# A list-scheduled two-layer trunk: new matmul durations and new priorities for the planner of the second layer's mixer

## The chip, the cores and the metric

The kernel runs on one core of a Trainium2 chip. The core has five engines that work side by side, each through its own queue in order: TensorE (PE in the profile; its weight loads are PEld), VectorE (DVE), ScalarE (ACT), GpSimd (POOL), and SyncE (SP), which here only issues DMAs. They meet through semaphores. The metric is the device time of one launch in microseconds (us).

## The reference

The reference is a trunk of two residual layers over 1024 tokens of width 1024, in float32. Cut to what matters here:

```python
# layer 0
x = x + short_conv_pool_mixer(rms_norm(x), ...)
x = x + swiglu(rms_norm(x), ...)                 # 1024 -> 2816 -> 1024
# layer 1
u = rms_norm(x) @ w_in_odd      # q, three k/v pairs (compressed, selected, window), gates, conformer a/b
o = g0*attn_compressed + g1*attn_selected + g2*attn_window   # 8 heads, 2 kv groups, 8 query blocks of 128
z = a * sigmoid(b)
z = causal_dwconv(z, 31 taps) + bias
z = silu(layer_norm(z))
x = x + concat(o, z) @ w_out_odd
x = x + swiglu(rms_norm(x), ...)
```

The first statement group of layer 1, up to the product with `w_out_odd`, is what this text calls the mixer. Its compressed branch also picks, for each query block, the key blocks that the selected branch may see.

## The kernel before, in words

The program does not issue its instructions as it goes. Every call on `nc.tensor`, `nc.vector` and so on is recorded by the class `Order` as an operation with a number (`seq`, in the order of the listing), the operations it depends on and the tiles that it touches. At the end `Order.order` plays the whole list through once, engine by engine, with a duration for every operation (`_cost`) and a latency for every hand-over (`LAT`), and `issue` writes the instructions in the order found. Among the operations of an engine that are ready in this play, the one with the lowest `grp` goes first. An engine is never left idle in the play when one of its operations is ready. On the chip each engine then follows its list strictly, whatever the real times are.

Counted in the order of the listing there are 14,699 operations: 0 to 5,825 are the first layer and the norm ahead of the second, 5,826 to 10,218 the mixer, 10,219 to 14,698 the output projection, the second FFN and the store. In the mixer `nc.at(name)` gives each part a phase name:

- `cf0` to `cf3`: conformer input of 128 of the 512 channels each, two products per half (`pcb`, `pca`), result `z31[i]`
- `pa`, `pb`, `pq`: the projections to keys and values (PSUM tiles `pa`, `pbk`) and to queries (`pcq`), and what follows them on DVE, ACT and POOL (tiles `ta`, `tb`, `tq`, `stq`)
- `cmp`: the compression of keys and values
- `conv00` to `conv32`: the depthwise convolution on DVE, one instruction of 128x1024 for each tap (here called a tap; in the trace `y<-z,dwv,y`), `conv<i><third>` for channel block i
- `prep<qb>`: for query block qb the transposed queries `QQ`, the compressed branch (`sc`, `pvc`) and the selection
- `smax<qb><g>`: scores `s` of one kv group, their row maxima on DVE (`mx`), then two small POOL operations that make `nmx`, a transpose on PE (`pm`) and four ACT copies into `QQ`
- `att<qb><g>`: transposed scores `sT`, the exponential on ACT (`pT`), and the product with the values (`pv`)
- `fin<qb>`: the block's result, transposed and split into `mB`
- `cn0` to `cn6`: layer norm and swish of the convolution. `cn0` starts with a sum over all four channel blocks (`sm`) and a product with ones (`mp`), so it needs every tap; `cn6` splits the result into `mB`
- `out`: everything after.

Two things bind the order besides the data. First, tiles of one tag share a few buffers, and the play hands these out in the order of recording, not of priority: the PSUM tag `ps` (tiles `pa`, `pbk`, `pcq`, `s`, `mp`, `vps`, `rb`, `po`) has two banks, `pa` (`sT`, `pcb`) and `pb` (`pv`, `pca`) two each, and the SBUF tag `whl` (split weights and `pT`) five. Recorded behind each other are `smax41`, `mp` of `cn0`, `smax50`, `vps` of `cn1`, `smax51`: while taps are left, `mp` holds one of the two `ps` banks, and when `smax50` has given up its last bank `vps` holds the other. Second, an engine's list is strict, so an operation that waits holds up all behind it.

The lines that the change touches:

```python
op.pe = passes, hold, free(st) / 1.2
t = passes * max(hold + 2.5, free(st) / 1.2)
...
op.grp = op.seq + self.shift.get(op.phase, 0)
...
op.occ = op.dur = passes * max(hold + 2.5, load)
```

Here `hold` is the number of columns that stream through, divided by 2.4 (doubled where the play believes the clock to be at half), and `load` the number of weight columns divided by 1.2.

Of the kernel before, what the change touches and what calls it, by code (L numbers as in the profile page):

```python
# [43 lines left out]
CONV_LAST = 3  # L44
START, START_V, START_C = 2, 2, 4

SHIFT = {'cf1': 672, 'pq': 801, 'cf0': -43, 'smax30': -3276, 'conv20': 3889, 'conv21': 2209, 'cf2': 214, 'smax10': -712, 'prep0': 671, 'out': 5314, 'att10': 125, 'conv30': 1208, 'att60': 401, 'pa': -123, 'att41': 2144, 'cn3': 559, 'prep3': 81, 'att00': 758, 'att20': 74, 'att50': 15, 'smax61': -584, 'cn6': -122, 'smax70': -1663, 'smax71': -431, 'prep4': -1373, 'prep5': -230, 'cf3': 62, 'smax41': -43, 'smax40': -415, 'pb': -643, 'att61': -370, 'conv31': 760, 'att40': -99, 'att11': -239, 'conv00': 672, 'smax60': -547, 'conv22': -411, 'prep7': -479, 'cn4': -662, 'conv11': -853, 'att31': 12, 'fin4': 99, 'cmp': -34, 'fin2': -837, 'att21': 14, 'conv32': -38, 'conv01': 474, 'prep1': -211, 'conv02': -231, 'prep6': -616, 'cn1': -173, 'smax11': -290, 'fin0': 159, 'smax31': 0, 'smax01': 291, 'smax00': 366, 'conv10': -65, 'smax21': -23, 'att30': -6, 'fin7': -512, 'cn2': -18, 'fin1': -250, 'fin5': -5, 'smax20': -14, 'att71': -10, 'smax50': 563, 'cn0': -98, 'smax51': -19, 'prep2': -65, 'cn5': 10, 'att01': -8, 'fin6': 65, 'att51': -116}


C_ID, C_A, C_B, C_COS, C_SIN, C_RATIO, C_M01, C_DEL, C_END = 0, 128, 192, 256, 512, 1024, 1088, 1152, 1156  # L50
# [61 lines left out]
class Order:  # L112
# [11 lines left out]
    SPAN = 4096 / 1.2  # L124
    PHASE = 0.0
    IDLE = 0.36

    def __init__(self, tc):
        self.tc = tc
        self.ops, self.bufs, self.tags, self.boxes = [], {}, {}, {}  # L130
        for e in ("tensor", "vector", "scalar", "gpsimd", "sync"):
            setattr(self, e, _Engine(self, e))
        self.shift = SHIFT
        self.phase = None
# [86 lines left out]
    def _cost(self, op, outs, ins):  # L221
        def free(ap):
            n = 1
            for st, k in list(ap.ap)[1:]:
                n *= k
            return n

        o, n = outs[0], free(outs[0])
        in_psum = any(str(a.space).endswith("PSUM") for a in ins + outs)
        ptr = sum(1 for a in ins if free(a) == 1 and n > 1)  # L230
        if op.eng == "sync":
            size = 1
            for st, k in list(o.ap):
                size *= k
            return 60.0, size * 4 / 280.0
        if op.eng == "tensor":
            st, mv = ins[0], ins[1]
            passes, hold = 1, free(mv) / 2.4
            if st.dtype == F32:
                hold *= 2  # L240
                passes = 2 if op.name == "matmul" else 1
            op.pe = passes, hold, free(st) / 1.2
            t = passes * max(hold + 2.5, free(st) / 1.2)
            return t, t
        if op.eng == "scalar":
            t = 0.833 * n + (51 if str(ins[0].space).endswith("PSUM") else 94) + 93 * ptr + (93 if op.kw.get("accum_out") is not None else 0)
            return t, t
        if op.eng == "vector":
            big = max([n] + [free(a) for a in ins])
            if op.name == "reciprocal":  # L250
                t = 6.0 * n + 69
            elif op.name in ("tensor_scalar", "tensor_copy", "memset") and not in_psum:
                t = 0.52 * big + 69 + 60 * ptr
            else:
                t = 1.042 * big + 69 + 60 * ptr
            return t, t
        if op.kw.get("op") == ALU.pow:
            t = 300 + 165.0 * n
        elif op.name == "tensor_tensor":
            t = 147 + 2.25 * n  # L260
        elif op.name == "memset":
            t = 38 + 0.83 * n
        else:
            t = (80 if n > 256 else 150) + 3.4 * n
        return t, t


    def order(self):
        import heapq

        engines = ("tensor", "vector", "scalar", "gpsimd", "sync")
        free = {e: 0.0 for e in engines}
        fut = {e: [] for e in engines}
        av = {e: [] for e in engines}
        dma = 0.0
        act_set = [None]
        slow, span_no, active = True, 0, 0.0
        sets = {AF.Exp: "e", AF.Tanh: "e", AF.Silu: "s", AF.Gelu_apprx_tanh: "g"}

        def push(op):  # L280
            est = 0.0
            for d in op.deps:
                est = max(est, d.end + self.LAT.get((d.eng, op.eng), self.WAIT))
            for b in op.tiles:
                est = max(est, b.avail)
            op.est = est
            heapq.heappush(fut[op.eng], (est, op.grp, op.seq, op))

        def ready(op):
            op.wait -= 1  # L290
            if op.wait == 0:
                push(op)

        def alloc(q):
            while q["next"] < len(q["queue"]) and q["free"]:
                b = q["queue"][q["next"]]
                q["next"] += 1
                b.avail = heapq.heappop(q["free"])
                for op in b.waiting:
                    ready(op)  # L300

        for q in self.tags.values():
            q["free"], q["next"] = [0.0] * q["n"], 0
        for b in self.bufs.values():
            b.avail, b.left, b.end, b.waiting = None if b.tag else 0.0, 0, 0.0, []
        for op in self.ops:
            op.users = []
            op.grp = op.seq + self.shift.get(op.phase, 0)
            for b in op.tiles:
                b.left += 1  # L310
        for op in self.ops:
            op.wait = 1 + len(op.deps)
            for d in op.deps:
                d.users.append(op)
            for b in op.tiles:
                if b.avail is None:
                    op.wait += 1
                    b.waiting.append(op)
        for q in self.tags.values():
            alloc(q)  # L320
        for op in self.ops:
            ready(op)
        out = []
        while len(out) < len(self.ops):
            best = None
            for e in engines:
                if av[e]:
                    t = free[e]
                elif fut[e]:
                    t = max(free[e], fut[e][0][0])  # L330
                else:
                    continue
                if best is None or t < best[0]:
                    best = (t, e)
            t, e = best
            while fut[e] and fut[e][0][0] <= t:
                x = heapq.heappop(fut[e])
                heapq.heappush(av[e], x[1:])
            op = heapq.heappop(av[e])[-1]
            if e == "scalar":  # L340
                g = sets.get(op.args[2] if len(op.args) > 2 else None)
                if g is not None and g != act_set[0]:
                    act_set[0] = g
                    t += 1283
            if e == "tensor":

                n = int((t + self.PHASE) / self.SPAN)
                while span_no < n:
                    slow = active < 0.765 * self.SPAN if slow else active < self.IDLE * self.SPAN
                    span_no, active = span_no + 1, 0.0  # L350
                passes, hold, load = op.pe
                if slow:
                    hold *= 2
                active += passes * hold
                op.occ = op.dur = passes * max(hold + 2.5, load)
            free[e] = t + op.occ
            if e == "sync":
                dma = max(dma, t + 1300) + op.dur
                op.end = dma + 500
            else:  # L360
                op.end = t + op.dur
            out.append((t, op))
            for b in op.tiles:
                b.end = max(b.end, op.end + (self.WAIT if b.tag else 0))
                b.left -= 1
                if b.left == 0 and b.tag is not None:
                    q = self.tags[b.tag]
                    heapq.heappush(q["free"], b.end)
                    alloc(q)
            for u in op.users:  # L370
                ready(u)
        self.span = max(op.end for op in self.ops)
        return [op for t, op in out]
# [19 lines left out]
def trunk(ctx, tc, x, norm_mix, norm_ffn, ffn_gate, ffn_up, ffn_down, w_in_even, conv_a, pool_w,  # L393
# [221 lines left out]
    def sums_a(r, name, U):  # L615
# [29 lines left out]
        yield  # L645

    def seven(U, B, name, order, out, small=False):


# [946 lines left out]
```

## Time and profile before

| | |
|---|---|
| median of 3 runs | 2278.22 us (2277.93 to 2279.83) |
| the profiled execution | 2277.39 us, of which 2275.6 us are the span from first to last instruction |
| PE, DVE, ACT busy in the span | 98%, 71%, 35% |
| mixer in the trace | about 990 to 1527 us |

Each row below comes from that one profiled execution. PE busy means that a matmul is in flight, so only the rest of a window is idle time of PE. PEclk is the granted share of TensorE's clock in the window: 1.00 is 2.4 GHz throughout, 0.50 would be 1.2 GHz throughout. A wait in square brackets is idle time of the engine just before that instruction, with what ended it.

### The profile page before, as it was taken

The numbers are of one execution on the slowest core, as the hardware profiler recorded it, in microseconds if no ns is written. First come the engines' busy times: TensorE is split into PE (matmuls) and PEld (weight loads), VectorE is DVE, ScalarE is ACT, GpSimd is POOL, SyncE is SP. The second block draws the span as 40 slices with busy tenths as digits, with TensorE's granted clock in tenths as the row PEclk, the third lists the DMA queues.
The fourth block names the chain that finished last, engine by engine and source line by source line (L and its number), as shares of the span: only waits on it lengthen the run. The fifth ranks groups of instructions, "written<-read, shape, count | busy, mean of one in ns | idle before, by whom it ended". The sixth has DMA issues, their size and how long they took to land.

```text
span 2275.6 us, 27709 instructions
## 1 busy us (share of the span) xinstructions
PE 2232.2 (98%) x10831; PEld 1844.6 (81%) x10831; DVE 1611.2 (71%) x2618; ACT 798.6 (35%) x1449; POOL 79.6 (3%) x116
## 2 busy tenths in 40 slices
PE   7999999999999999999999999999999999999999
PEld 6888878888888888878887887988788888888887
DVE  6444387777777467769999998833877777774674
ACT  4222263333333212324334434641633333332220
POOL 0000000000000000101121000000000000000000
PEclk9999999999999999999999998999999999999999
DMA  5113123444437864313200000031223535368652
GB/s 173 55 56 139 65 75 109 144 154 138 167 123 278 328 236 163 126 55 92 75 19 1 1 1 1 29 121 56 84 102 122 184 120 178 128 240 325 238 195 93
DMA packets 171403, 283.93 MB, mean 125 GB/s; under 512 B 7120, under 2 KB 127880, under 8 KB 157448
## 3 DMA queue, kind: packets, MB, share of 16 engines
q1 hardware_dynamic: 171272, 282.16, 35.0%
q8 instruction: 85, 1.39, 0.3%
q14 instruction: 46, 0.38, 0.1%
HBM read 195.10 MB, written 87.03 MB: 124 GB/s over the span
## 4 chain that ended last, share of the span: by engine, by line
PE 91%; DVE 5%; ACT 1%; issue 1%; POOL 0%; DMA 0%; SPq 0%; POOLq 0%; ACTq 0%; DVEq 0%
PE pd L379 19%; PE pg L379 18%; PE pu L379 18%; PE po L379 8%; PE pv L379 4%; PE s L379 3%; PE sT L379 3%; PE pvv L379 2%; PE pp L379 2%; PE pb L379 2%; PE pcc L379 2%; PE pcq L379 2%; PE pca L379 2%; PE pcb L379 1%; PE pn L379 1%; PE pbk L379 1%
## 5 line engine op out<-in xcount | busy, mean ns | idle before, releaser
L379 PE MATMUL pd<-tw,sl 128*128 128x512 f32 x1512 | 349.7, 393 | 0.0
L379 PEld LDWEIGHTS pd<-tw,sl 128*128 128x128 f32 x1512 | 284.2, 188 | 65.2
L379 DVE SCALAR_TENSOR_TENSOR y<-z,dwv,y 128x1024 f32<-128x1024 f32 x120 | 154.1, 1284 | 0.8
L379 PEld LDWEIGHTS pv<-V,pT 128*128 128x128 f32 x1056 | 142.8, 193 | 6.6 <-ACT pT L379 0.6
L379 DVE TENSOR_TENSOR xf<-pd,xf 128x512 f32<-128x512 f32 x128 | 86.4, 690 | 81.6 <-PE pd L379 81.1
L379 ACT CAST tw<-wdr 128x512 fp32r<-128x512 f32 x108 | 63.8, 620 | 222.2 <-PE pd L379 202.8
L379 PE MATMUL pv<-V,pT 128*128 128x65 f32 x1056 | 138.9, 267 | 0.1
L379 PE MATMUL pg<-T,wgc 128*128 128x512 f32 x528 | 131.0, 395 | 3.1 <-ACT T L379 1.6
L379 PE MATMUL pu<-B,wua 128*128 128x512 f32 x528 | 132.3, 393 | 0.0
L379 PE MATMUL pg<-B,wga 128*128 128x512 f32 x528 | 130.4, 393 | 0.0
L379 PE MATMUL pu<-T,wuc 128*128 128x512 f32 x528 | 128.7, 392 | 0.0
L379 PEld LDWEIGHTS pg<-T,wgc 128*128 128x128 f32 x528 | 100.0, 190 | 27.2 <-ACT T L379 2.5
L379 DVE TENSOR_TENSOR tw<-wdr,tw 128x512 fp32r<-128x512 f32 x108 | 71.5, 689 | 68.4 <-ACT tw L379 68.1
L379 ACT CAST sa<-act 128x512 fp32r<-128x512 f32 x108 | 64.0, 622 | 154.4 <-PE pu L379 68.6
L379 PEld LDWEIGHTS pu<-B,wua 128*128 128x128 f32 x528 | 99.1, 188 | 23.1
L379 PEld LDWEIGHTS pg<-B,wga 128*128 128x128 f32 x528 | 98.8, 188 | 22.5
L379 PEld LDWEIGHTS pu<-T,wuc 128*128 128x128 f32 x528 | 99.1, 188 | 22.1
L379 ACT ACTIVATE pT<-sT 128x512 f32<-128x512 f32 x132 | 77.4, 598 | 102.5 <-PE sT L379 101.6
L379 DVE TENSOR_TENSOR act<-pg,pgu 128x512 f32<-128x512 f32 x66 | 45.6, 691 | 82.7 <-PE pg L379 82.6
L379 DVE TENSOR_REDUCE mx<-s 128x2 f32<-128x512 f32 (+3 forms) x160 | 93.1, 594 | 11.3 <-PE s L379 8.8
L379 DVE TENSOR_TENSOR puu<-pu,puu 128x512 f32<-128x512 f32 x88 | 60.7, 690 | 50.6 <-PE pu L379 48.9
L379 PE MATMUL pd<-wd,ah 128*128 128x512 f32 x384 | 91.5, 395 | 0.0
(364 smaller groups left out, 4455.1 us busy)
## 6 DMA issues: line engine op xcount, KB each, us to landing
sd<-sa SPq DMA_DIRECT2D x54, 1024.0 KB, 4.2
sl<-sd SPq DMA_DIRECT2D x54, 1024.0 KB, 8.2
raw<-in_ffn_gate_dram SPq DMA_DIRECT2D x44, 512.0 KB, 4.8
rawp<-in_ffn_up_dram SPq DMA_DIRECT2D x40, 512.0 KB, 4.0
wdr<-in_ffn_down_dram SPq DMA_DIRECT2D x18, 1024.0 KB, 6.5
sd<-sa SPq DMA_DIRECT2D x18, 512.0 KB, 2.6
sl<-sd SPq DMA_DIRECT2D x18, 512.0 KB, 3.8
raw<-in_w_in_even_dram SPq DMA_DIRECT2D x16, 512.0 KB, 4.3
```

Source lines behind the costliest of these rows:

```text
L379: getattr(getattr(nc, op.eng), op.name)(*op.args, **op.kw)
```

## The change

Three things in `Order`, and no change in what is computed, in the tiles or in their buffers.

1. Durations of matmuls in the play. `RATE = 13 / 12` multiplies the streaming time where 2.5 ns were added before, and 4 ns are added to the weight load.
2. `grp` takes a second shift, for the pair of phase and engine, beside the one for the phase. A phase can now stand early on one engine and late on another.
3. The table `SHIFT` is replaced: 73 entries between -3,276 and 5,314 become 321, with sums for a phase and an engine between about -39,000 and 36,000. Phases outside the mixer other than `out` have no entry, before or after.

```diff
-SHIFT = {'cf1': 672, 'pq': 801, 'cf0': -43, 'smax30': -3276, 'conv20': 3889, 'conv21': 2209, ...}
+SHIFT = {
+    'att00': 5710, ('att00', 'tensor'): -7918, ('att00', 'vector'): -16911, ('att00', 'scalar'): -4221,
...
+    'att40': 23737, ('att40', 'tensor'): 7673, ('att40', 'vector'): 1545, ('att40', 'scalar'): -9967,
...
+    ('cn0', 'vector'): -524, ('cn0', 'scalar'): 3810, 'cn1': -3645, ('cn1', 'tensor'): -18813,
...
+    ('conv01', 'vector'): 6881, 'conv02': -5626, ('conv02', 'vector'): -3017, 'conv10': 29102,
+    ('conv10', 'vector'): 6674, 'conv11': 25052, ('conv11', 'vector'): -5225, 'conv12': 13445,
+    ('conv12', 'vector'): -3632, 'conv20': 17215, ('conv20', 'vector'): 169, 'conv21': 6508,
+    ('conv21', 'vector'): 15471, 'conv22': 27248, ('conv22', 'vector'): 660, 'conv30': 6553,
+    ('conv30', 'vector'): 24326, 'conv31': 23142, ('conv31', 'vector'): 12555, 'conv32': 3929,
...
+}
@@
     IDLE = 0.36
+    RATE = 13 / 12
@@
-            op.pe = passes, hold, free(st) / 1.2
-            t = passes * max(hold + 2.5, free(st) / 1.2)
+            op.pe = passes, hold, free(st) / 1.2 + 4
+            t = passes * max(hold * self.RATE, op.pe[2])
@@
-            op.grp = op.seq + self.shift.get(op.phase, 0)
+            op.grp = op.seq + self.shift.get(op.phase, 0) + self.shift.get((op.phase, op.eng), 0)
@@
-                op.occ = op.dur = passes * max(hold + 2.5, load)
+                op.occ = op.dur = passes * max(hold * (1 if slow else self.RATE), load)
```

With the recording numbers added, nine of the twelve tap phases stand on DVE at 15,089 to 44,285 (`conv10` 43,367, `conv31` 44,285), `conv00` and `conv01` at 10,014 and 12,192, `conv02` at -1,062. Of the 16 `smax` phases 13 stand below 15,000 on DVE; `smax50`, `smax51` and `smax61` stand at 21,141, 19,771 and 31,328. The DVE part of `cn0` stands at -13,529. Before, the numbers of the taps ran from about 6,700 to 11,900, among those of the `smax` phases.

## Rows read from the trace of the kernel before

**Rows 1.** The page: busy time by engine; DVE busy and PE clock in 40 slices.

```profile
PE 2232.2 (98%) x10831; PEld 1844.6 (81%) x10831; DVE 1611.2 (71%) x2618; ACT 798.6 (35%) x1449; POOL 79.6 (3%) x116
...
DVE  6444387777777467769999998833877777774674
...
PEclk9999999999999999999999998999999999999999
```

**Rows 2.** Busy time of each engine by stretch; the first line names the columns.

```profile
core 0: us, PE busy (x) PEld busy (x) DVE busy (x) ACT busy (x) POOL busy (x), PEclk, DMA share, GB/s
...
990.00:1060.00 70.00, 67.08 (x329) 52.35 (x328) 65.99 (x169) 27.50 (x86) 6.87 (x9) 1.00 0.18 54
1060.00:1200.00 140.00, 138.09 (x731) 116.36 (x731) 131.85 (x197) 45.88 (x219) 26.90 (x24) 1.00 0.20 56
1200.00:1310.00 110.00, 106.06 (x782) 93.01 (x780) 103.24 (x241) 50.50 (x117) 9.92 (x20) 1.00 0.00 1
1310.00:1390.00 80.00, 71.69 (x455) 61.15 (x454) 70.16 (x136) 33.13 (x63) 7.17 (x7) 0.89 0.00 1
1390.00:1490.00 100.00, 100.00 (x721) 92.41 (x721) 79.52 (x201) 55.72 (x104) 4.62 (x12) 1.00 0.09 29
1490.00:1527.00 37.00, 37.00 (x270) 33.34 (x270) 12.40 (x36) 18.75 (x29) 0.00 (x0) 1.00 0.45 151
...
1620.00:1660.00 40.00, 36.21 (x155) 28.66 (x154) 35.44 (x45) 20.90 (x28) 0.86 (x1) 0.96 0.23 66
```

**Rows 3.** What PE waited for, 1060 to 1527: us in total, times, longest.

```profile
PE pm L379 <- POOL nmx L379: 6.0, 3, 3.4
PE sT L379 <- ACT pT L379: 2.2, 3, 1.0
PE pqt L379 <- ACT QQ L379: 1.5, 2, 1.2
```

**Rows 4.** The same for 990 to 1060, the projection to keys and values.

```profile
PE pk L379 <- DVE ta L379: 1.3, 5, 0.6
PE pt L379 <- DVE ta L379: 1.1, 6, 0.2
```

**Rows 5.** The chain that ended last, 1361 to 1370: start us, us, what.

```profile
1361.89 1.19 DVE y L379
...
1363.55 1.19 DVE y L379
...
1364.95 1.19 POOL nmx L379
...
1366.21 1.28 POOL nmx L379
...
1367.54 0.34 PE pm L379
```

**Rows 6.** The same chain: two long runs of equal matmuls, with their counts.

```profile
1152.44 35.69 PE pcq L379 x154
...
1472.40 6.20 PE pv L379 x56
```

**Rows 7.** Tile nmx: ns min/median/max, first and last start us.

```profile
L379 POOL CAST nmx<-mx x16: 189/192/1211, 1202.8 to 1487.2; 128x8 fp32r<-128x8 f32 x16
L379 POOL TENSOR_TENSOR nmx<-mx,nmx x16: 201/202/1272, 1203.1 to 1487.5; 128x8 f32<-128x8 f32 x16
```

**Rows 8.** Tiles y, mp and mB, same columns: taps, first product of the norm, last split.

```profile
L379 DVE SCALAR_TENSOR_TENSOR y<-z,dwv,y x120: 1239/1279/2062, 999.3 to 1377.0; 128x1024 f32<-128x1024 f32 x120
...
L379 PE MATMUL mp<-sm,ones x4: 592/594/647, 1383.1 to 1402.8; 128*128 128x512 f32 x4
...
L379 DVE TENSOR_TENSOR mB<-y,mB x8: 681/686/693, 1452.8 to 1485.6; 128x512 fp32r<-128x512 f32 x8
```

**Rows 9.** What DVE waited for most, 1060 to 1390.

```profile
DVE QQ L379 <- ACT QQ L379: 10.7, 10, 3.9
```

**Rows 10.** What PE waited for most, 1610 to 1700, the second FFN's start.

```profile
PE pg L379 <- DVE pgu L379: 2.2, 1, 2.2
```

More of the change, by code (lines that the diff above doesn't have):

```diff
@@ L45 @@
 START, START_V, START_C = 2, 2, 4
-SHIFT = {'cf1': 672, 'pq': 801, 'cf0': -43, 'smax30': -3276, 'conv20': 3889, 'conv21': 2209, 'cf2': 214, 'smax10': -712, 'prep0': 671, 'out': 5314, 'att10': 125, 'conv30': 1208, 'att60': 401, 'pa': -123, 'att41': 2144, 'cn3': 559, 'prep3': 81, 'att00': 758, 'att20': 74, 'att50': 15, 'smax61': -584, 'cn6': -122, 'smax70': -1663, 'smax71': -431, 'prep4': -1373, 'prep5': -230, 'cf3': 62, 'smax41': -43, 'smax40': -415, 'pb': -643, 'att61': -370, 'conv31': 760, 'att40': -99, 'att11': -239, 'conv00': 672, 'smax60': -547, 'conv22': -411, 'prep7': -479, 'cn4': -662, 'conv11': -853, 'att31': 12, 'fin4': 99, 'cmp': -34, 'fin2': -837, 'att21': 14, 'conv32': -38, 'conv01': 474, 'prep1': -211, 'conv02': -231, 'prep6': -616, 'cn1': -173, 'smax11': -290, 'fin0': 159, 'smax31': 0, 'smax01': 291, 'smax00': 366, 'conv10': -65, 'smax21': -23, 'att30': -6, 'fin7': -512, 'cn2': -18, 'fin1': -250, 'fin5': -5, 'smax20': -14, 'att71': -10, 'smax50': 563, 'cn0': -98, 'smax51': -19, 'prep2': -65, 'cn5': 10, 'att01': -8, 'fin6': 65, 'att51': -116}
+SHIFT = {
[22 rows of a table added]
+    'cmp': 2894, ('cmp', 'tensor'): -9886, ('cmp', 'vector'): -4638, ('cmp', 'scalar'): 15532,
+    ('cmp', 'gpsimd'): -3391, ('cmp', 'sync'): -1056, 'cn0': -21914, ('cn0', 'tensor'): 6074,
[20 rows of a table added]
+    ('fin7', 'scalar'): -6175, 'out': -11783, ('out', 'tensor'): 1102, ('out', 'vector'): -5708,
+    ('out', 'scalar'): 4378, ('out', 'gpsimd'): -9183, ('out', 'sync'): 5380, 'pa': 5781,
[37 rows of a table added]
+}
 C_ID, C_A, C_B, C_COS, C_SIN, C_RATIO, C_M01, C_DEL, C_END = 0, 128, 192, 256, 512, 1024, 1088, 1152, 1156
```

71 rows, old and new, of the table SHIFT are left out of this document.

## The prediction

> **What bounds the kernel now.** I read the page first. PE is busy 98% of the span, at full clock in every slice but one, and DVE is at nine tenths just where the mixer lies [rows 1]. So the kernel is bound by PE, and a new order can win back at most the time in which PE stands idle or runs at half clock. The busy times by stretch say how much that is and where [rows 2]. Idle time of PE is the window less its busy time: 70 - 67.08 = 2.9 us in 990 to 1060, 1.9 in 1060 to 1200, 3.9 in 1200 to 1310, 8.3 in 1310 to 1390, and nothing from 1390 to 1527. Together 17.1 us. The granted clock of 0.89 over the 80 us from 1310 means that (1 - 0.89) / 0.5 = 22% of them, 17.6 us, went at 1.2 GHz; everywhere else in the mixer it is 1.00. Of these slow us I take 3 as idle, from the gaps named below, so the other 14.6 lost half, 7.3 us. The mixer thus gives away 24.4 us, 1.1% of the kernel. That is the ceiling for this change in the mixer. The start of the second FFN has 3.8 us of idle time more and 0.08 x 40 = 3.2 us at half clock, 1.6 lost.
>
> Next I asked what ends these gaps. In the attention part the largest is the transpose `pm`, which waits for POOL's `nmx`: 6.0 us in three waits; then `sT` for the exponentials 2.2 and `pqt` for ACT 1.5 [rows 3]. In the key/value projection it is many short waits for DVE's `ta` [rows 4]. The chain shows the worst `pm` in detail [rows 5]: a maximum, a tap of 1.19, a maximum, a tap of 1.19, then two POOL operations of 1.19 and 1.28, then `pm` at 1367.54. From 1368 on PE runs slowly on little work.
>
> Why has PE nothing else just there? Because of the order in which the PSUM banks are handed out. `mp` needs every tap. The last tap starts at 1377.0, and `mp` runs at 1383.1 [rows 8]. Until then `mp` holds one bank of tag `ps` and `vps` the other, so `smax51` can't begin, and PE uses up what is left of `att50` and `prep`. So up to about 1383 the stretch is bound by DVE, which must get all its taps done, and PE is only nearly full. DVE is busy 65.99 + 131.85 + 103.24 + 70.16 = 371.2 of the 400 us from 990 to 1390 [rows 2]: it has 28.8 us of idle time ahead of that gate.
>
> **The durations.** The old plan prices a product of 512 columns at 512/2.4 + 2.5 = 215.8 ns, the new one at 213.3 x 13/12 = 231.1. The trace has 35.69 us for 154 of them, 231.8 each. One pass of `pv` was 106.7 (its weight load) and becomes 110.7; the trace has 6.20/56 = 110.7 [rows 6]. So the new prices are the real ones. The old plan held PE's work too short by 4 to 15.3 ns an instruction, which over the 2,297 matmuls of 990 to 1390 [rows 2] makes 9 to 35 us. No instruction gets faster by this. What changes is the order on the other engines: with PE's and ACT's results expected too early, DVE's list puts operations that wait for them ahead of taps that could run. The row for that is DVE's wait for ACT's copy of `QQ`, 10.7 us in ten waits, one of 3.9 [rows 9]. Behind each of them stand taps, and behind the taps the gate.
>
> The Trainium skill, in "TensorE: Matmul & The Clock Gate", section "Wait — 56ns, not 53.3ns?", speaks against this part: it gives N/2.4 GHz plus about 2.5 ns for a warm matmul, 215.7 ns at 512 columns, which is the old plan's price. By it the new plan would hold PE's work 7% too long and these 10.7 us would not come back; the sum below would be about 0. The trace has 231.8 at a granted clock of 1.00, and the measurement decides.
>
> **The priorities, DVE.** Nine of twelve tap phases now stand behind 13 of 16 `smax` phases; before, the two ran mixed. A maximum that is ready then goes before any tap, and a wait as in [rows 5] loses the two taps in front, 2 x 1.19 = 2.4 us, as an upper bound; the lower bound is nothing, where the maximum isn't ready. It costs DVE nothing, since the same operations run. The gate doesn't get later by it as long as DVE is never idle, because everything else that DVE could do first was already done by then. `cn0` stands ahead of all this (-13,529), so the sum follows the last tap at once; today it takes 1383.1 - 1378.3 = 4.8 us from the end of the last tap to `mp` [rows 8], with little in it to win.
>
> **The priorities, PE, ACT, POOL, SP.** PE's shifts are larger than the whole mixer (4,393 operations), but most of their freedom is taken by the tags: `sT`, `s`, `pv` and the weights keep the order of recording. `pq` stands far ahead of `cf2` on PE, for example, yet its four weight tiles come behind those of `cf2` and `cf3` in `whl`, which has five buffers; so it can't move ahead. What can move is how far `smax` runs ahead of `att`: `att10` to `att31` and `att40` stand late and are left to fill gaps. That decides when PE runs dry ahead of the gate, not how much it has to do before it. Its value lies between 0 and the 8.3 us of 1310 to 1390; I count nothing of it by itself. SP's queue moves only loads of weights that wait for buffers anyway; the window of 1200 to 1390 has no DMA at all [rows 2], so I count 0, and either way no more than the 1.9 us that PE idles from 1060 to 1200. Outside the mixer only the prices change. PE has no idle time in most of that, and the wait at the second FFN's start, 2.2 us [rows 10], is DVE's; 0, within 4 us either way.
>
> **The sum.** The gate comes earlier by what DVE gets back. I take the 10.7 us of [rows 9], because that is the wait that the wrong prices explain; the ends are 0 and 28.8 us of DVE's idle time. PE's loss shrinks with it, from 24.4 to 13.7, most of it out of the 8.3 + 7.3 = 15.6 us at 1310 to 1390. Of the waits in [rows 4], 2.4 us, I take half, 1.2. Against it I set one new wait, below. POOL's pair takes 0.19 + 0.20 alone and about 1.2 each beside a tap [rows 7]; one pair more that PE waits for is 2.1 us, half of which I count: 1.0. The sum is -10.7 - 1.2 + 1.0 = -10.9 us. The profiled execution is 2277.39, 0.8 under the median of 2278.22; from the median, 2278.2 - 10.9 gives 2267.
>
> **Rivals.** (a) Slower, by POOL. Its two operations are priced in both plans near their short durations, and neither plan knows that a tap beside one makes it 1.2 us [rows 7]. With taps behind everything else, a tap starts just when the last maximum of a `smax` is done, that is when `nmx` is due; with PE's times now exact the plan also loses the slack of 7% that let PE come late to `pm`. If each of the eleven `pm` up to the gate then waits 2.1 us and each brings a fall of the clock as in 1620 to 1660 (3.2 us, 1.6 lost), the mixer gives away 11 x 3.7 = 41 us instead of 24.4: 2278 + 16 = 2294. It decides from seven waiting `pm` on (7 x 3.7 = 26); today three wait. For it speaks [rows 5]; against it that 13 of 16 `pm` now come without a wait. Half of it would give about 2286.
>
> The Trainium skill, "SBUF — State Buffer", section "Who interferes with whom", has the rule behind (a): a VectorE instruction with two inputs in SBUF shuts out a GpSimd instruction that reads SBUF for its whole length. The trace agrees, with 189 ns alone and 1211 beside a tap; by the rule no priority helps while taps are left.
>
> (b) Slower, by a late gate. If DVE takes up work that isn't due before the gate (its share of 1390 to 1527 is 91.9 us [rows 2]) ahead of the taps, the gate and the norm behind it move. The last split starts at 1485.6 [rows 8] and the output projection needs it by about 1527, so up to 40 us are covered; 60 us of such work would give 2278 + 20. The tags leave little of it within reach.
>
> (c) No difference. DVE stays the bound ahead of the gate at the same 371 us, other waits take the place of [rows 9], and PE's 24.4 us only change their place: 2278 within 4.6.
>
> (d) More than forecast: PE's order also closes the dry stretch, and all 24.4 us go: 2254.
>
> **How the numbers follow.** The forecast's neighbourhood, 2258 to 2273, has 0.54 and (d), below 2258, 0.10; (c) has 0.15; (a) 0.17 and (b) 0.04. The range goes from (d)'s 2254, with half of (d) beyond it, to half of (a) at 2287, with 0.10 beyond it. A measurement of this kernel tells a change of 0.2%, 4.6 us, from none. So faster 0.64, same 0.15, slower 0.21.
>
> **What would show it.** Right: the granted clock from 1310 to 1390 back near 1.00; the last tap and `mp` some 10 us earlier; DVE's wait for ACT's `QQ` down to a few us; no pair of taps ahead of a maximum that `pm` waits for. Matmul durations and counts must be the same. Wrong: seven waits or more of `pm` for `nmx` (a); `mB<-y` ending after the first rows of `po` want it (b); DVE's busy time ahead of `mp` unchanged and PE idle by 17 us at other places (c). The forecast is wrong at its root if PE's gaps don't follow the gate at all.

## The result, and the profile after

| | median, us | ratio to before, 95% interval |
|---|---|---|
| before | 2278.07 | 1 |
| after the change | 2290.91 | 1.0059 [1.0047, 1.0071] |

The change makes the kernel 12.8 us slower, outside the range that was predicted (2254 to 2287). The profiled execution of after took 2292.52 us, 2290.7 of them span. One execution, of the kernel called table alone below, took 2779.14 us at a granted clock of 0.747 and is left out of its median.

Busy times by stretch, after; the columns are those of [rows 2], and the last stretch is longer because the mixer now ends later:

```profile
990.00:1060.00 70.00, 64.89 (x316) 49.84 (x315) 67.90 (x171) 24.53 (x84) 5.58 (x8) 1.00 0.14 43
1060.00:1200.00 140.00, 137.48 (x723) 113.87 (x722) 125.37 (x194) 48.39 (x223) 24.28 (x21) 1.00 0.20 58
1200.00:1310.00 110.00, 104.19 (x712) 89.74 (x711) 100.10 (x226) 45.55 (x108) 12.64 (x23) 0.95 0.00 1
1310.00:1390.00 80.00, 76.86 (x519) 68.47 (x518) 75.08 (x148) 34.25 (x66) 4.87 (x8) 0.96 0.00 1
1390.00:1490.00 100.00, 99.18 (x648) 90.27 (x648) 62.62 (x165) 45.58 (x83) 3.73 (x10) 0.92 0.00 1
1490.00:1542.00 52.00, 52.00 (x362) 46.97 (x362) 21.21 (x54) 22.15 (x39) 0.39 (x2) 1.00 0.36 128
```

Idle time of PE adds up to 5.1 + 2.5 + 5.8 + 3.1 + 0.8 + 0 = 17.3 us, as much as the 17.1 of before, but in other places: the dry stretch from 1310 to 1390 (dry: PE has nothing that it could run) has 3.1 us instead of 8.3. The clock differs. Time at 1.2 GHz, called time at half rate from here on, is (0.05 x 110 + 0.04 x 80 + 0.08 x 100) / 0.5 = 33.4 us, against 17.6 before. And it no longer lies where PE is idle: from 1390 to 1490 PE is busy 99.18 of 100 us and 16 of them go at half rate.

The gate came earlier, as forecast. Tiles y and mp, columns as in [rows 8], and DVE's wait for ACT in 1060 to 1390:

```profile
L464 DVE SCALAR_TENSOR_TENSOR y<-z,dwv,y x120: 1255/1280/2067, 989.2 to 1371.2; 128x1024 f32<-128x1024 f32 x120
...
L464 PE MATMUL mp<-sm,ones x4: 592/592/595, 1375.2 to 1431.6; 128*128 128x512 f32 x4
...
DVE QQ L464 <- ACT QQ L464: 5.7, 11, 0.7
DVE stq L464 <- ACT tq L464: 5.7, 2, 3.5
```

`mp` runs at 1375.2, 7.9 us earlier than in [rows 8], and the wait of [rows 9] has halved. But DVE has a new wait of the same size for ACT's `tq`. Its busy time from 990 to the start of the last tap, before and after:

```profile
990.00:1377.00 387.00, 369.92 (x2214) 312.07 (x2213) 359.87 (x716) 150.62 (x473) 50.86 (x58) 0.98 0.11 31
```

```profile
990.00:1371.20 381.20, 366.66 (x2167) 307.01 (x2166) 353.16 (x705) 142.54 (x460) 45.32 (x56) 0.99 0.10 30
```

DVE is idle for 27.1 us there before and for 28.0 us after. So the gate didn't come earlier because DVE waits less; DVE has 6.7 us less work to do ahead of it, which now stands elsewhere in its list. With the prices alone (the first run below) both move, idle time to 22.3 us and work to 355.6.

What PE does around the three falls of the clock, two stretches each, one ahead and one within:

```profile
1277.00:1283.00 6.00, 5.45 (x40) 4.48 (x39) 4.74 (x8) 4.51 (x8) 0.00 (x0) 1.00 0.00 0
1284.00:1294.00 10.00, 10.00 (x44) 9.32 (x44) 7.57 (x19) 2.28 (x4) 0.00 (x0) 0.50 0.00 0
1376.00:1382.00 6.00, 4.68 (x33) 3.76 (x32) 5.57 (x12) 5.89 (x12) 0.00 (x0) 1.00 0.00 0
1383.00:1393.00 10.00, 10.00 (x42) 9.43 (x43) 5.75 (x11) 2.30 (x4) 1.01 (x1) 0.50 0.00 0
1431.00:1437.00 6.00, 5.19 (x34) 3.87 (x32) 4.62 (x14) 5.10 (x9) 0.00 (x0) 1.00 0.00 0
1438.00:1451.00 13.00, 13.00 (x54) 12.42 (x55) 8.27 (x17) 3.67 (x7) 1.38 (x1) 0.50 0.00 1
```

Ahead of each fall PE is busy for 78 to 91% of the time, and within it all the time. PE's timeline at the second fall (start us, us, engine, line, operation, count):

```profile
1380.49 0.50 PE L464 MATMUL sT<-QQ,K1s 128*128 128x512 f32 x1 [0.77 <-ACT pT L464]
1380.83 0.55 PE L464 MATMUL pv<-V,pT 128*128 128x65 f32 x4
1381.21 0.38 PE L464 MATMUL sc<-cb 128*128 128x512 bf16 x1
1381.24 2.33 PE L464 MATMUL sc<-Kc,QQ 128*128 128x64 f32 x16
1383.38 1.10 PE L464 MATMUL pv<-V,pT 128*128 128x65 f32 x4
1384.23 0.77 PE L464 MATMUL sT<-QQ,K2s 128*128 128x512 f32 x1
1384.81 1.80 PE L464 MATMUL pv<-V,pT 128*128 128x65 f32 x8
```

All three falls look like this: short waits for the exponential (0.55 us at 1281, 0.56 and 0.77 at 1377 and 1380, 0.36 at 1434), then 16 products `sc` of 64 columns in one go, with `pv` of 65 columns around them. Such a product takes some 110 ns whether it streams 65 columns or 112 (measured below), so PE is busy but streams little. The clock falls while the `sc` run. From there eight `pv` passes take 1.80 us, against 1.00 us for eight at 1277.88, at full clock.

### The profile page after: what moved, and what is told of

It is laid out like the page before. It is cut to its first block, busy times and chain, and to the rows that moved or that the text cites. A ratio compares the mean times of both kernels' runs of the same rounds, so it can differ in the third digit from the quotient of the medians.

```text
span 2290.7 us, 27749 instructions
## 1 busy us (share of the span) xinstructions
PE 2248.1 (98%) x10831; PEld 1852.8 (81%) x10831; DVE 1607.2 (70%) x2618; ACT 796.9 (35%) x1449; POOL 75.3 (3%) x116
## 4 chain that ended last, share of the span: by engine, by line
PE 87%; DVE 8%; ACT 2%; issue 1%; DMA 1%; POOL 0%; SPq 0%; ACTq 0%; DVEq 0%; POOLq 0%
PE pd L464 19%; PE pg L464 18%; PE pu L464 18%; PE po L464 7%; PE pv L464 4%; PE sT L464 3%; PE s L464 3%; PE pvv L464 2%; PE pp L464 2%; PE pb L464 2%; PE pcc L464 2%; PE pcq L464 2%; DVE y L464 1%; PE pn L464 1%; PE pca L464 1%
## 5 line engine op out<-in xcount | busy, mean ns | idle before, releaser
L464 PEld LDWEIGHTS pv<-V,pT 128*128 128x128 f32 x1056 | 149.4, 200 | 9.3 <-ACT pT L464 2.4
L464 PE MATMUL pv<-V,pT 128*128 128x65 f32 x1056 | 144.2, 274 | 1.5 <-ACT pT L464 0.9
L464 PE MATMUL po<-woo,mB 128*128 128x512 f32 x384 | 92.7, 397 | 0.0
L464 PE MATMUL po<-woe,mA 128*128 128x512 f32 x384 | 91.2, 395 | 0.1
```

The costliest lines, as they stand in the source:

```text
L464: getattr(getattr(nc, op.eng), op.name)(*op.args, **op.kw)
```

## The experiments

Two families were tried: the change taken apart, and the prices in the plan nudged (moved by an amount that means nothing), to see what in the plan makes the time; and the orders kept as they are with more columns per product, to see what the clock makes. Times are medians beside runs of before on the same chip.

| kernel | median, us | before, us | ratio, 95% interval |
|---|---|---|---|
| prices alone | 2290.60 | 2277.36 | 1.0055 [1.0040, 1.0070] |
| table alone | 2312.25 | 2277.36 | 1.0159 [1.0137, 1.0180] |
| after, pv 112 wide | 2278.43 | 2277.36 | 1.0003 [0.9994, 1.0013] |
| before, pv 112 wide | 2276.70 | 2277.36 | 0.9996 [0.9987, 1.0006] |
| before, nudged by 0.5 ns | 2287.34 | 2277.72 | 1.0046 [1.0031, 1.0061] |
| load price alone | 2297.79 | 2277.72 | 1.0087 [1.0072, 1.0102] |
| streaming price alone | 2298.76 | 2277.72 | 1.0094 [1.0074, 1.0114] |
| prices alone, pv 112 wide | 2289.65 | 2277.72 | 1.0051 [1.0034, 1.0068] |
| after, pv 112 wide, longer hand-over | 2289.46 | 2277.25 | 1.0052 [1.0038, 1.0066] |
| after, nudged | 2289.24 | 2277.25 | 1.0052 [1.0038, 1.0066] |
| before, pv 112 wide, waits filled | 2273.79 | 2277.25 | 0.9984 [0.9975, 0.9993] |
| after, pv 88 wide | 2280.37 | 2277.25 | 1.0016 [1.0005, 1.0027] |
| nudged, pv 112 wide | 2286.72 | 2277.40 | 1.0040 [1.0025, 1.0055] |
| load price alone, pv 112 wide | 2294.27 | 2277.40 | 1.0073 [1.0056, 1.0090] |

**Prices alone.** The new `RATE` and weight load with the old table.

> Only the new matmul prices, with the old table of shifts. Theory of the prediction (right prices take DVE's waits for ACT and PE away and the gate comes earlier): about 2268 us, DVE's wait for ACT's QQ from 10.7 to a few us in the mixer, last tap some 10 us earlier. Rival (the old table was chosen for the old prices, and every other set of prices gives it an order that was chosen for nothing): 2278 or slower, with half-rate time of PE's clock above the 17 us of before.

2290.60 us: the rival's time and, with 28 us at half rate in the mixer, its sign. The prices alone cost all that the change costs. Yet the gate moved: `mp` runs at 1371.1. The stretches:

```profile
1310.00:1390.00 80.00, 72.81 (x462) 63.88 (x462) 72.02 (x141) 31.77 (x61) 7.33 (x8) 0.89 0.00 1
1390.00:1490.00 100.00, 96.37 (x649) 86.34 (x648) 71.95 (x177) 51.88 (x95) 2.62 (x10) 0.97 0.06 17
```

PE is dry ahead of the gate as before (7.2 us, clock 0.89), and now also idles 3.6 us behind it, where before it had none.

**Table alone.** The new shifts with the old prices:

```diff
     # as before: max(hold + 2.5, free(st) / 1.2)
-            op.grp = op.seq + self.shift.get(op.phase, 0)
+            op.grp = op.seq + self.shift.get(op.phase, 0) + self.shift.get((op.phase, op.eng), 0)
```

> Only the new table of shifts, by phase and by engine, with the old prices. If the table makes the loss: 2290 us or slower, with some 34 us at half clock as after the change. If prices and table only go together (the table was chosen under the new prices): clearly slower than after the change, 2295 to 2310 us. If the prices make the loss: near 2278 us.

2312.25 us, just above what was expected if prices and table only go together, with 63 us at half rate in the mixer. With old table and old prices the kernel takes 2278, with new prices 2291, with the new table 2312, with both 2291: under the new prices the new table is worth nothing over the old one; under the old prices it costs 35 us.

**After, wide.** The changed kernel with `pv` streaming 112 of V's columns. The plan still prices the product of 65 columns, and the wide one takes its place once the operation is recorded, so all five orders are the same:

```diff
-                pv = psb([P, R, HD + 1], "pv")
+                pw_ = psb([P, R, 112], "pv")
+                x0 = (0, 47)[g]
+                pv = pw_[:, :, x0:x0 + 65]
...
-                                 start=kb == k0 and r == 0, stop=kb == qb and r == R - 1)
+                                 start=kb == k0 and r == 0, stop=kb == qb and r == R - 1,
+                                 wide=(pw_[:, r], V[:, br, kb, 64 * g - x0:64 * g - x0 + 112]))
...
+        if wide is not None:
+            op.args = (wide[0], args[1], wide[1])
```

> The changed kernel with every engine's order as it is; each pass of the product pv streams 112 columns of V instead of 65 (the added columns land beside the result and are read by nobody). At full clock a pass is bound by its weight load, 110.7 ns, so this costs nothing there; PE only does more in the same time. Theory A (the loss is the clock: 34 us at half rate against 17, 9.4 us of added matmul time): the half-rate time falls to under 12 us and the kernel to about 2279 us. Rival B (the clock falls because PE waits for other engines, and the waits make the loss): half-rate time stays near 30 us, the kernel at 2289 us or above; with the clock falling as before, a pass at half rate would even take about 190 ns instead of 120, so up to 2298 us.

2278.43 us: theory A, to the microsecond of its estimate; the ten executions lie between 2277.80 and 2281.71. The stretches, and the same place on PE's timeline as above:

```profile
1200.00:1310.00 110.00, 103.91 (x741) 89.13 (x740) 103.97 (x232) 47.27 (x111) 11.88 (x22) 1.00 0.00 1
1310.00:1390.00 80.00, 77.19 (x542) 68.46 (x541) 76.73 (x158) 34.29 (x66) 5.65 (x8) 1.00 0.00 1
1390.00:1490.00 100.00, 99.22 (x696) 90.91 (x695) 62.86 (x164) 50.10 (x93) 3.02 (x9) 0.98 0.00 1
```

```profile
1376.32 2.06 PE L467 MATMUL sc<-Kc,QQ 128*128 128x64 f32 x16
1378.21 0.68 PE L467 MATMUL pv<-V,pT 128*128 128x112 f32 x4
1378.65 0.47 PE L467 MATMUL sT<-QQ,K2s 128*128 128x512 f32 x1
1378.97 1.04 PE L467 MATMUL pv<-V,pT 128*128 128x112 f32 x8
```

Time at half rate is 0.02 x 100 / 0.5 = 4 us instead of 33.4. Idle time of PE in these three stretches is 6.1 + 2.8 + 0.8 = 9.7 us against 5.8 + 3.1 + 0.8 = 9.7: the waits are all still there. So these 12.5 us are the clock's and not the waits'. (The estimate of 120 ns for a pass of 65 columns at half rate, in the price of rival B, is too low: the eight above take 1.80 us.) The 47 columns more cost nothing at full rate; the longest run of `pv` in each chain, after and after wide:

```profile
1526.14 4.41 PE pv L464 x40
```

```profile
1511.86 4.45 PE pv L467 x40
```

One thing doesn't fit yet. After wide has 4 us at half rate in the mixer where before has 17.6, and no more idle time (2276.3 - 2233.4 = 42.9 us in the whole span, against 2275.6 - 2232.2 = 43.4); it should be faster than before by some 7 us and isn't. PE's busy time, after, after wide, table alone, and the wide product with the prices alone:

```profile
PE 2248.1 (98%) x10831; PEld 1852.8 (81%) x10831; DVE 1607.2 (70%) x2618; ACT 796.9 (35%) x1449; POOL 75.3 (3%) x116
```

```profile
PE 2233.4 (98%) x10831; PEld 1839.7 (81%) x10831; DVE 1606.5 (71%) x2618; ACT 797.2 (35%) x1449; POOL 74.7 (3%) x116
```

```profile
PE 2257.1 (98%) x10831; PEld 1865.6 (81%) x10831; DVE 1615.0 (70%) x2618; ACT 797.3 (35%) x1449; POOL 72.3 (3%) x116
```

```profile
PE 2238.9 (98%) x10831; PEld 1842.7 (81%) x10831; DVE 1605.8 (70%) x2618; ACT 797.2 (35%) x1449; POOL 74.9 (3%) x116
```

Less half of the time at half rate, an estimate of what PE's work takes at full clock is 2231 us for after, 2231 for after wide, 2232 for the wide product with the prices alone, 2226 for table alone, and 2232.2 - 8.9 = 2223 for before (the prediction's 7.3 and 1.6 us). The same products take PE 5 to 8 us longer in these plans with the new prices than in the two with the old ones. Why stays open. A wait that ends while the product ahead of it is still in flight counts as busy time, so it could be short waits; no row shows it.

**Before, wide.** The same edit in the kernel before.

> The same widening of pv in the kernel before, order unchanged. Before spends 17 us of the mixer at half rate, 13.7 of them behind a stretch of 5 us in which PE had run dry, which no width of pv can fill. Theory A: the 3.4 us at 1313 go, the 13.7 stay: 2276 to 2277 us. Rival B: 2278 us or slightly above.

2276.70 us; the interval holds no change. As expected the fall behind the dry stretch stays, where there is nothing to widen, and with it 14.4 us at half rate. The other 3.2 us of before's 17.6, from a fall at 1313, are gone:

```profile
1310.00:1390.00 80.00, 71.80 (x464) 61.56 (x463) 71.70 (x143) 32.80 (x62) 7.16 (x7) 0.91 0.00 1
```

**A nudge, and the two prices one by one.** Each is an edit of the kernel before, with its old table; the second `max` in `order` is changed in the same way:

```diff
# nudge
-            t = passes * max(hold + 2.5, free(st) / 1.2)
+            t = passes * max(hold + 3.0, free(st) / 1.2)
# load price alone
+            t = passes * max(hold + 2.5, free(st) / 1.2 + 4)
# streaming price alone
+            t = passes * max(hold * 13 / 12, free(st) / 1.2)
```

> The kernel before with its fixed cost of a matmul in the plan at 3.0 ns instead of 2.5, old table: a nudge of 0.5 ns of no meaning, towards the measured price. Theory L (the old table was chosen for its prices to the nanosecond; any other price gives an order that nobody chose): as slow as with the new prices alone, 2284 to 2296 us, with more than 25 us at half clock. Theory P (the new prices take slack out of the plan and so are worse by themselves): a nudge does little, 2275 to 2282 us.

> The kernel before with only the 4 ns more for a weight load in the plan (pv, sc and other narrow products), old table. Theory L: 2284 to 2296 us. Theory P: the smaller part of the price change, under a third of the +13 us: 2278 to 2282 us.

> The kernel before with only the factor 13/12 for streaming time in the plan, old table. Theory L: 2284 to 2296 us, like any other price. Theory P: most of the +13 us of the prices, 2287 to 2291 us, with PE's waits for ta in 990 to 1060 at 5 us as with both prices, against 2.4 before.

2287.34, 2297.79 and 2298.76 us: nearer to theory L, the last two just above its range. Half a nanosecond in the price of a matmul costs 9.6 us, and neither price by itself is better than both. The three plans tried near that of before are slower by 10 to 21 us. The stretch ahead of the gate doesn't set them apart: in the nudge it has 10.4 us idle and 0.11 x 80 / 0.5 = 17.6 us at half rate, before had 8.3 and 17.6. The nudge has another 11 us at half rate from 1200 to 1310, in its profiled execution of 2291.70 us:

```profile
1200.00:1310.00 110.00, 106.44 (x752) 94.31 (x751) 98.99 (x234) 48.76 (x114) 10.01 (x23) 0.95 0.00 1
1310.00:1390.00 80.00, 69.65 (x439) 59.45 (x437) 69.93 (x131) 28.60 (x56) 6.22 (x6) 0.89 0.00 1
```

One part of theory P holds all the same. PE's waits for `ta` in 990 to 1060 with prices alone and after, where [rows 4] has 2.4 us:

```profile
PE pt L380 <- DVE ta L380: 3.0, 8, 0.5
PE pk L380 <- DVE ta L380: 2.5, 8, 0.4
```

```profile
PE pt L464 <- DVE ta L464: 2.8, 7, 0.5
PE pk L464 <- DVE ta L464: 2.3, 8, 0.4
```

Every kernel with the old streaming price (before, nudge, load price, table alone) has 2.1 to 2.8 us there, every one with the new streaming price 4.9 to 5.6, whatever its table.

**The wide product in other plans.** Orders kept, `pv` 112 wide, for prices alone, the nudge and the load price.

> New prices with the old table (2290.6 us, 27 us at half clock, 12.3 us of matmul time added by it), order as it is, pv streaming 112 columns instead of 65. Theory A (the clock makes the loss): its half-rate time falls to under 15 us and the time to 2280 to 2284 us; idle time of PE, 23.5 us against 17.4 before, stays and keeps it above before. Rival B (waits make the loss and the clock follows): 2288 us or above.

> The plan of the nudge by 0.5 ns (2287.3 us; 34 us at half clock, 27 of them in the attention part), every order as it is, pv 112 columns wide instead of 65. Theory A (most plans lose by PE's clock where narrow products come together): under 15 us at half clock in the mixer and 2279 to 2282 us. Rival W (waits of PE make the loss; its idle time in the mixer is 5 us above before): the clock recovers in part and the time stays at 2285 us or above, as with the new prices alone.

> The plan with only the price of a weight load changed (2297.8 us; 37 us at half clock), every order as it is, pv 112 columns wide. Theory A: under 15 us at half clock in the mixer and 2284 to 2288 us. Rival W: 2294 us or above.

2289.65, 2286.72 and 2294.27 us. Theory A fails here: the wide product gave 12.5 us to the changed kernel, but 1.0, 0.6 and 3.5 to these. The stretch ahead of the gate in the wide nudge and in the wide prices alone:

```profile
1310.00:1390.00 80.00, 69.81 (x438) 59.52 (x436) 70.61 (x136) 30.80 (x59) 6.21 (x6) 0.87 0.00 1
```

```profile
1310.00:1390.00 80.00, 72.09 (x466) 63.08 (x465) 72.09 (x142) 31.92 (x62) 5.98 (x7) 0.91 0.00 1
```

The fall behind the dry stretch stays in both, as in the wide kernel before: 20.8 and 14.4 us at half rate there, and 10.2 and 7.9 us idle, against 14.4 and 8.2. For the nudge that is a part of its loss. For the prices alone it is none, since the wide kernel before has the same and is 13 us faster. Their loss lies in idle time of PE in the rest of the mixer (23.5 us in all, against 16.9 in the wide kernel before) and in the longer busy time at full clock named above. The clock is thus the main loss of the changed kernel, but not of every slow plan.

**A longer hand-over.** To give slack back, the plan of after (wide) takes 600 ns for a hand-over from DVE to PE instead of 245.

```diff
-           ("vector", "tensor"): 245.0
+           ("vector", "tensor"): 600.0
```

> The changed kernel with pv 112 columns wide, and in the plan a hand-over from DVE to PE of 600 ns instead of 245, which gives back the slack that the exact streaming price took out. The time isn't the test here (it is a new plan, and a new plan loses its table). Theory S (exact prices leave PE too close behind DVE): PE's waits for ta in 990 to 1060 fall from 5 us to 2.5 or less, the value of all kernels with the old streaming price. Rival (those waits come from the table): they stay at 5 us. Time: 2280 to 2295 us.

PE's waits for `ta` stay at 5.2 us (2.7 + 2.5). Theory S, in this form, falls: a longer hand-over in the plan doesn't bring the old order of that stretch back. Why the new streaming price makes these waits is left open.

**After, nudged.** `RATE` of 1.0857 instead of 1.0833.

> The changed kernel with the factor 1.0857 instead of 13/12 = 1.0833, half a nanosecond for 512 columns. Theory L (each table fits its own prices alone): slower than after the change by 5 to 25 us, 2296 to 2316 us, as the same nudge cost the kernel before 9.6 us. If the new table, with its choice by part and engine, is sturdier than the old: 2288 to 2294 us.

2289.24 us, the same as after. One nudge doesn't prove it, but theory L in its general form isn't borne out: here the new table doesn't hang on its prices to the nanosecond. The plans tried under the new prices, whole, in part or nearly, lie at 2289 to 2299 us with either table; it is the order of before that stands out.

**Filling the dry stretch of before.** `pv` 112 wide, and 26 products that nobody reads, ahead of four instructions that PE waits at:

```diff
+                    if op.name == "transpose" and name.startswith("pm"):
+                        pm += 1
+                        n = 14 if pm == 11 else 0
+                    elif pm == 11 and name.startswith("pqt"):
+                        n = 5 if st == 0 else 0
+                        st = max(st, 1)
+                    elif pm == 11 and 1 <= st and name.startswith("sT"):
+                        n = {3: 4, 5: 3}.get(st, 0)
+                        st += 1
+                for _ in range(n):
+                    nc.tensor.matmul(*self.extra[0], **self.extra[1])
...
+                nc.extra = (mp, identb, cb[:, 0:512]), dict(start=True, stop=True)
```

> The kernel before with pv 112 columns wide and 26 products of 512 columns that nobody reads, put on PE just ahead of the four waits at 1362 to 1372 (14, 5, 4, 3 of them, about 0.23 us each, no longer than the waits). They go into the bank that mp holds unused. All other orders as before. If the half-rate clock makes PE's loss there: the 13.7 us at half rate go and the kernel takes 2270 to 2273 us. If the gate (last tap, mp at 1381) binds: the clock stays up, PE is done sooner and waits longer for mp, and the time is 2275 to 2277 us.

2273.79 us, faster than both kernels: 0.9984 [0.9975, 0.9993] of before. The stretch, the first fill and what follows it, and the place of `mp`:

```profile
1310.00:1390.00 80.00, 75.13 (x510) 62.39 (x509) 73.84 (x152) 33.49 (x64) 7.66 (x8) 1.00 0.01 1
```

```profile
1362.37 3.19 PE L396 MATMUL mp<-cb 128*128 128x512 bf16 x14
1365.85 0.33 PE L397 MATMUL pm<-cf,nmx 128*128 128x128 f32 x1 [0.29 <-POOL nmx L397]
...
1378.63 0.65 PE L397 MATMUL ptc<-cf,ecmp 128*128 128x128 f32 x4 [1.40 <-ACT ecmp L397]
1379.12 1.02 PE L397 MATMUL mp<-sm,ones 128*128 128x512 f32 x2
```

The 17.6 us at half rate are gone, and `mp` runs at 1379.1 against 1383.1 in [rows 8]. The time lies just above the first expectation and below the second: of the 7.3 us that the prediction counted for the slow time, some 3 us show. Part of the rest is a new wait of 1.4 us, of `ptc` for ACT's `ecmp`, just ahead of `mp`. DVE makes that `ecmp` behind the last taps, so the gate may well bind here, but no run isolates it.

**A smaller dose.** After with `pv` 88 columns wide.

> The changed kernel with pv 88 columns wide, between the 65 of the change and the 112 of the earlier run (34.1 and 3.4 us at half clock, 2290.9 and 2278.4 us). Theory A: in between in both, 7 to 27 us at half clock and 2280 to 2287 us. If the width helped for another reason than the clock (such as where the product lies in its bank): 2278 us like the wide one, whatever the clock does.

2280.37 us, but the ten executions differ: five take 2276.32 to 2278.65 us with a mean granted clock of 0.997 to 0.999, five 2282.08 to 2287.76 us with 0.995 to 0.998. The profiled one, 2278.01 us, is of the first kind; there the clock stands at 0.98 from 1390 to 1490 and at 1.00 from 1200 to 1390, as with 112 columns. So 88 columns keep the clock up in some executions and not in others, with the same orders and the same width, and the time goes with the clock.

## Why the prediction was wrong

**What held.** The reading of before: idle and slow time of PE. The prices, for the products that the trace shows as f32: `pv` keeps its 110 ns a pass, and the longest run of `pcq` after takes 17.17 us for 74, 232 ns each. For products in bf16 they are not exact: the fills above start 216 ns apart, which is the old plan's price. PE's order closed the dry stretch, which the forecast had only as (d), from 8.3 to 3.1 us idle. DMA showed nothing, as forecast.

**What held in its number alone.** The gate: forecast 10.7 us earlier, measured 7.9. The forecast had DVE's idle time shrink by 10.7 us; it went from 27.1 to 28.0 us, with 5.0 us less of the wait for `QQ` and a new wait of 5.7 us for `tq`. The gate moved because 6.7 us of DVE's work no longer stand ahead of it, which was no term of the sum.

**The step that failed** is the first sentence of the sum's second half: "PE's loss shrinks with it, from 24.4 to 13.7". The gate came earlier and PE's loss grew. I read the half-rate time of [rows 2] as a part of the dry stretch, since both stood in the same row, and concluded that it would go when the idle time went. The idle time did go from that place, though not from the mixer (17.3 against 17.1 us). But the clock fell in three places with PE busy for 78 to 91% of the time just ahead, where it ran 16 `sc` in one go beside `pv` and short waits. Time at half rate went from 17.6 to 33.4 us. Nearly all of that passes with PE busy, so half of it is lost: 16.7 us against the 7.3 of before. PE's idle and slow time in the mixer is thus 34.0 us where the forecast had 13.7. The run with the wide product shows the clock as a cause, not as a companion: all orders kept, the same waits, and 12.5 us gone.

The clock is about half of the 15.1 us by which the span grew (2290.7 against 2275.6). It costs 16.7 us in place of 7.3 and, at the start of the second FFN, 1.6. Idle time over the whole span is about the same, 42.6 against 43.4 us. The other 8 us, by subtraction, are PE's longer busy time at full clock. The sum had that at nothing, and what it is stays open; it goes with the new prices and not with the table.

**The rivals.** (a) would have covered the measured time, with 2294, but by another mechanism, and that one didn't come: `pm` waited for `nmx` twice, 2.6 us in all, instead of three times and 6.0, so the sum's 1.0 us for one wait more didn't come either. Nor is it so that no priority helps while taps are left: of the eleven casts `nmx<-mx` ahead of the gate five took over 1.1 us before, and two after. (b) didn't come either: the last split moved from 1485.6 to 1554.1, 68 us, but PE has no idle time from 1490 to 1542. (c) came in its mechanism, other waits in place of [rows 9] and PE's idle time in other places; its price left out the clock and the 8 us.

**The second failure** is about the prices. I took an exact price for a gain, worked out from one wait that it should remove. It removed half of that wait, the waits for `ta`, of which I took 1.2 us off, rose from 2.4 to 5.1 us, and the prices by themselves cost 13 us. That the list of before was an unusually good one among its neighbours is suggested by three plans, no more: a change of 0.5 ns, with no meaning at all, cost 9.6 us. The profile of one execution could not show this, but it could have been priced as a rival: every order near this one is unknown, and the known one leaves PE no idle time at all from 1390 to 1527 [rows 2].

**The rival that was missing** reads: the clock falls where narrow products meet short waits, though PE hardly stands still; 34 us instead of 17. It could have been seen in the trace of before. In [rows 2] the windows from 1200 and from 1390 have a matmul for every 141 and 139 ns, against 231.8 for a wide one, and two of the three falls after lie there. And of the two falls in the mixer of before one came with PE at work for 4.84 of the 6 us ahead, behind one wait of 1.42 us at 1313:

```profile
1307.00:1313.00 6.00, 4.84 (x37) 4.42 (x35) 6.00 (x10) 1.80 (x3) 2.24 (x2) 1.00 0.00 0
```

## What to carry to other kernels

For a PE that is nearly always busy, look at columns streamed per microsecond beside idle time: here the clock halved at runs of narrow products with no wait longer than 0.8 us beside them. A narrow product could be made wider for nothing at full clock (65 to 112 columns), and a wait on PE could be filled with products that nobody reads, as long as they end before the wait does. Read the executions one by one: at 88 columns the same kernel kept its clock in some and lost it in others. A list schedule tuned by hand is one draw among many; correcting the planner's prices throws that draw away, so a better model has to win back the luck first.

## What the runs showed of the hardware

- TensorE's granted clock fell to 1.2 GHz with PE busy 91%, 78% and 87% in the 6 us ahead, and stood at 0.50 through the next windows of 10, 10 and 13 us, in which PE was busy throughout. With `pv` of 112 columns in place of 65, the same orders and the same idle time, all but 4 of 33.4 us at 1.2 GHz were gone.
- A pass of `pv` with 112 columns instead of 65 took 4.45/40 = 111 ns against 4.41/40 = 110 ns at full clock; eight with 65 columns took 1.80 us at 1.2 GHz and 1.00 us at 2.4.
- 14 products of 512 columns in bf16 took 3.19 us at a granted clock of 1.00, from the first start to the last end. One takes 379 ns from start to end, so they start (3190 - 379) / 13 = 216 ns apart; those of 512 columns that the trace shows as f32 take 231.8 ns each [rows 6].

```profile
L396 PE MATMUL mp<-cb x14: 379/379/379, 1362.4 to 1365.2; 128*128 128x512 bf16 x14
```
